# Dense matmuls of a two-layer encoder issued in uninterrupted runs

## The chip, the cores and the metric

The kernel runs on one core of a Trainium2 chip. The metric is device time in microseconds (us) for one execution: the median of three runs of the kernel before is 2465.99 us (2465.27 to 2466.29). Smaller is better.

## The reference

The program is an encoder of two layers over 1024 frames of 1024 channels, in float32. Layer 0 projects the normed input with one matrix (`w_in`), gives one half of the columns to a recurrent mixer (RWKV-7, 8 heads of 64) and the other to a banded attention (8 heads of 64), joins the two and projects back. Layer 1 is a convolution module. Each layer ends in a squared-ReLU feed-forward block (FFN) of width 4096. Cut to what matters here:

```python
h = rmsnorm(x, norm_mix)
proj = h @ w_in                                  # 1024 x 3328
p_rwkv, q, k, v = split(proj)
y = concat([rwkv7_group(p_rwkv, ...), chunk_band_attention(q, k, v, rel_bias)])
x = x + y @ w_out
x = x + square(relu(rmsnorm(x) @ up)) @ down     # 1024 -> 4096 -> 1024
# inside rwkv7_group, one step for each of 1024 frames:
sa = S @ (-kk_t)
S  = S * w_t + outer(sa, kk_t * a_t) + outer(v_t, k_t)
y_t = S @ r_t
```

The feed-forward blocks and the projections are large and independent matmuls. The recurrence is a chain: each block of 64 frames needs the state that the block before it left.

## The kernel before

**Tiles.** Activations lie channel by frame, in tiles of 128 channels by 512 frames, so the 1024 frames are two halves (0 and 1). A product with a weight matrix is made of dense steps, each one matmul of a 128x128 weight block with a 128x512 activation tile. Weights and activations are split in a high and a low part, and `gemm` (L273 to L275) issues three matmuls for each block: high by high, high by low, low by high. One output tile takes 8 blocks, so 24 dense matmuls into one PSUM bank. The column block for the attention's values (L367 to L369) uses four banks at once. In all there are 8,976 dense matmuls; below they are counted from the start of the program.

**Weights.** Each part of four blocks is loaded on SyncE's queue (`wr`, L213), cast on ScalarE (`wh`, L217) and subtracted on VectorE (`wl`, L218). In the mixed stage there are four buffers of each, one part serves 12 dense matmuls.

**The mixed stage.** Mixer and attention consist of small matmuls with ScalarE and VectorE steps between them. They are interleaved on TensorE with dense work that doesn't depend on them. The first part runs mixer and attention of half 0 beside `w_in_gemm` of half 1 (dense matmuls 625 to 1248). The second part runs mixer and attention of half 1 beside `mixer_out` and `ffn` of half 0 (1249 to 2976). Then the pools change and the wide stage begins with `glu`; it holds no mixer and no attention. Before the mixed stage lies `w_in_gemm` of half 0 (1 to 624), with the transposes of the input (L311).

**The mixer's lines.** `prep` (L478 on: low-rank matmuls L481 and L482, head sums L442 and L449, L534, L547), `stage2` (L638, L645, the inverse L609 and L621), and `chain`. Chain does for each 64 frames three matmuls in one bank `c`, each of which needs the one before it by way of ScalarE and VectorE: L667, then `zs` (L669, L670), L671, then `uv` (L672, L673), L677, then the state (L680), and again L667. Then come L687, L691 and `finish` (L442, L449, L713). Attention has L791 and L793 (scores), L813 (transposes) and L820 (values). Results go through DRAM tiles `yd` (L715, L824) and are read by `mixer_out` into `mh` (L867).

**What sets the order.** A scheduler places the instructions of all engines before the program runs. On each engine it takes, of what it holds to be ready, the instruction with the lowest priority number. Each kind of work counts up from a level of its own:

```python
level = {"support": 1_000, "mixer": 1_000_000, "attn": 2_000_000, "dense": 3_000_000}
```

So weight preparation and evacuations (`boost()`) go first, then the mixer, then attention, and a dense matmul is placed only where nothing else is held to be ready. The engines then run these fixed orders; an instruction that isn't ready holds up all that stand behind it on its engine.

Of the kernel before, what the change touches and what calls it, by code (L numbers as in the profile page):

```python
# [14 lines left out]
P = 128  # L15
# [3 lines left out]
KT = 8  # L19
KH = 4  # L20
# [31 lines left out]


LINE = 32


def whole(n):
    return -(-n // LINE) * LINE


@with_exitstack
def encoder_trunk(ctx: ExitStack, tc: tile.TileContext, x, vecs, consts, ext, w2a2, g2, w_in, w_out,
                  up0, dn0, pw1, pw2, up1, dn1, out):
    nc = tc.nc
# [15 lines left out]
    def psum(tag):  # L80
        return ps[tag].tile([P, T], F32, tag=tag, name=tag)
# [53 lines left out]
    yd = [dram.tile([P, SEQ], F32, tag=f"yd{i}", name=f"yd{i}") for i in range(KT)]  # L135
    xd = [[dram.tile([P, T], F32, tag=f"xd{h}_{i}", name=f"xd{h}_{i}") for i in range(KT)] for h in range(2)]

    level = {"support": 1_000, "mixer": 1_000_000, "attn": 2_000_000, "dense": 3_000_000}

    class At:  # L140
        def __init__(self, name):
# [6 lines left out]
        def __exit__(self, *a):  # L148
            level[self.name] = tc.cur_priority
            tc.cur_priority = self.save  # L150

    def boost():
        return At("support")
# [72 lines left out]
    def gemm(w, row0, mts, rhs, evac, st=None, first=(), taper=False, after=None, halves=False):  # L226
        mts = list(mts)
        step = 2 if wide[0] else 1
        units = [(mts[i : i + step], ALL) for i in range(0, len(mts), step)]
        late = st if wide[0] and st is not None and st.r is None else None  # L230
        if late is not None and len(units) > 2:
            units[2:3] = [([m], ALL) for m in units[2][0]]
        if taper:
            cuts = (slice(0, T // 2), slice(T // 2, T)) if halves else (ALL,)
            units[-1:] = [([m], c) for c in cuts for m in units[-1][0]]
        held, late_m, loaded = [], [], {}

        def tail():
            with boost():
                for m, c in late_m:  # L240
                    after(m, c)
            late_m.clear()

        def flush():
            with boost():
                for m, c, q in held:
                    evac(m, q, c)
            held.clear()

        def get(m):  # L250
            if m not in loaded:
                loaded[m] = weights(w, row0, m)
            return loaded[m]

        for i, (grp, cols) in enumerate(units):
            with boost():
                ws = [first[i]] if i < len(first) else [get(m) for m in grp]
            qs = [psum(SPARE[i] if first and i < len(SPARE) else "d") for _ in grp]
            for k in range(KT):
                if i == 1 and k == 6 and late is not None:  # L260
                    with boost():
                        late.spread()
                    flush()
                if k == KT // 2:
                    while deferred:
                        deferred.pop(0)()
                    if late_m:
                        tail()
                xh, xl = rhs[k]
                with At("dense"):  # L270
                    for q, parts in zip(qs, ws):
                        hi, lo = (a[:, k % KH, :] for a in parts[k // KH])
                        nc.tensor.matmul(q[:, cols], hi, xh[:, cols], start=(k == 0), stop=False)  # L273
                        nc.tensor.matmul(q[:, cols], hi, xl[:, cols], start=False, stop=False)  # L274
                        nc.tensor.matmul(q[:, cols], lo, xh[:, cols], start=False, stop=(k == KT - 1))  # L275
            held += [(m, cols, q) for m, q in zip(grp, qs)]
            if i == 0 and late is not None:
                with boost():
                    late.sums()
            else:  # L280
                flush()
            if after is not None:
                late_m += [(m, cols) for m in grp]
        if late_m:
            deferred.append(tail)
# [52 lines left out]
    def w_in_gemm(h, rhs, st, first=()):  # L338
        def evac(m, q, cols):
            rstd = st.rstd()  # L340
            s = tmp("t1")
            if Q0 <= m < K0:
                nc.vector.scalar_tensor_tensor(out=s[:], in0=q[:], scalar=0.125, in1=rstd[:],
                                               op0=ALU.mult, op1=ALU.mult)
            else:
                nc.vector.tensor_tensor(out=s[:], in0=q[:], in1=rstd[:], op=ALU.mult)
            ts = slice(h * T, (h + 1) * T)
            if Q0 <= m < V0:
                hi = tmp("t2")
                nc.scalar.copy(hi[:].bitcast(F32R), s[:])  # L350
                nc.vector.tensor_tensor(out=s[:].bitcast(F32R), in0=s[:], in1=hi[:], op=ALU.subtract)
                nc.gpsimd.dma_start(ph[m][:, ts], hi[:])
                nc.gpsimd.dma_start(pl[m][:, ts], s[:])
            else:
                nc.gpsimd.dma_start(pd[m][:, ts], s[:])

        gemm(w_in, 0, IN_ORDER, rhs, evac, st, first)
        qs = [psum(tag) for tag in SPARE]
        for k in range(KT):
            with boost():  # L360
                hi, lo = (a[:].rearrange("p a b -> p (a b)")
                          for a in weight_part(w_in[k * P : (k + 1) * P, V0 * P : V0 * P + RW], RW))
            xh, xl = rhs[k]
            with At("dense"):
                for t, q in enumerate(qs):
                    ts = slice(t * P, (t + 1) * P)
                    nc.tensor.matmul(q[:], xh[:, ts], hi, start=(k == 0), stop=False)  # L367
                    nc.tensor.matmul(q[:], xl[:, ts], hi, start=False, stop=False)
                    nc.tensor.matmul(q[:], xh[:, ts], lo, start=False, stop=(k == KT - 1))  # L369
        with boost():  # L370
            for t, q in enumerate(qs):
                s = tmp("t1")
                nc.scalar.activation(s[:], q[:], AF.Copy, scale=st.part[1][:, t : t + 1])
                nc.gpsimd.dma_start(vd[h * T + t * P : h * T + (t + 1) * P, :], s[:])
# [487 lines left out]
    def mixer_out(h, xs, mp):  # L862
        with boost():
            rhs = []
            for k in range(KT):
                t = mp.tile([P, T], F32, tag="mh", name="mh")
                nc.sync.dma_start(t[:], yd[k][:, h * T : (h + 1) * T])  # L867
                rhs.append(split(t[:], k))
        st, nrhs, last = norm_collect(xs, "g1")
        residual_gemm(w_out, 0, rhs, xs, last=last)  # L870
        return nrhs, st
# [152 lines left out]
    with banks(d=2, w=2, v=1, c=1, a=2), tc.tile_pool(name="lop", bufs=1) as lop, tc.tile_pool(name="wp1", bufs=4) as wb[0]:  # L1024
# [7 lines left out]
        with tc.tile_pool(name="xrp", bufs=4, reuse_waits="tile") as xrp:  # L1032
# [17 lines left out]
            for i in range(8):  # L1050
                t = dram.tile([P, EXTW + 1], F32, tag=f"ext{i}", name=f"ext{i}")
# [13 lines left out]
        with tc.tile_pool(name="mp", bufs=8, reuse_waits="tile") as mp, tc.tile_pool(name="rp2", bufs=1, reuse_waits="tile") as rp, tc.tile_pool(name="ap2", bufs=1, reuse_waits="tile") as ap:  # L1065
            with At("mixer"):
                rwkv(1, rp, 2)
            with At("attn"):
                attention(1, ap)
            r, s = mixer_out(0, xa, mp)  # L1070
            r, s = ffn(xa, r, s, up0, dn0, mp, "g2")
            stash_x(0, xa)

    wide[0] = True
    with banks(d=5, w=1, o=2), tc.tile_pool(name="wp2", bufs=8, reuse_waits="tile") as wb[0], tc.tile_pool(name="mp2", bufs=10, reuse_waits="tile") as mp, tc.tile_pool(name="sx", bufs=4, reuse_waits="tile") as extra[0], tc.tile_pool(name="up", bufs=1, reuse_waits="tile") as up:
        dwt = up.tile([P, KT * TAPS], F32, tag="dwt", name="dwt")
        nc.scalar.dma_start(dwt[:], vecs[:, VOFF["dw"] : NVEC])
        halo = up.tile([P, KT, TAPS - 1], F32, tag="halo", name="halo")
        nc.gpsimd.memset(halo[:], 0.0)
        us = glu(0, r, s, up)  # L1080
        with At("mixer"):
            ca, sca = conv(us, up)
        with boost():
            xb = fetch_x(1)
        r, s = mixer_out(1, xb, mp)
        r, s = ffn(xb, r, s, up0, dn0, mp, "g2", late=lambda: conv_norm(ca, sca, up))
        stash_x(1, xb)
        us = glu(1, r, s, up)
        with boost():
            xa = fetch_x(0)  # L1090
        r, s = pw2_block(ca, xa)
        with At("mixer"):
            cb, scb = conv(us, up)
        o = Out(0, xa, up, False)
        ffn(xa, r, s, up1, dn1, mp, None, o, late=lambda: conv_norm(cb, scb, up))
        deferred.append(o.finish)
        with boost():
            xb = fetch_x(1)
        r, s = pw2_block(cb, xb)
        ffn(xb, r, s, up1, dn1, mp, None, Out(1, xb, up, True))  # L1100
        deferred.pop()()
# [69 lines left out]
```

## Time and profile before

| | |
|---|---|
| median of three runs | 2465.99 us |
| the profiled execution's own time | 2465.91 us |
| its span (first to last instruction) | 2463.8 us |
| TensorE (PE) busy | 2425.1 us (98%) |
| weight loads on TensorE (PEld) busy | 1963.6 us (80%) |
| VectorE (DVE) busy | 1709.4 us (69%) |
| ScalarE (ACT) busy | 1192.7 us (48%) |
| clock granted to TensorE, mean | 0.996 of full |

All times of the trace count from the start of the span. Dense matmul 625 starts at 235 us, number 1249 at 499 us, 2017 (the first after the last matmul of mixer or attention) at 865 us, and 2977 (the wide stage) at 1083 us. A matmul's bar ends by a model: in a stream of dense matmuls a bar is 0.39 us long and the next one starts 0.23 us after it, so the step from start to start is the time that counts. A matmul of float32 operands shows as two (x2) where it isn't a transpose.

### The profile page before, as it was taken

To read this page: it belongs to the slowest core of one execution; us is meant where nothing else is said; L and a number is where in the kernel's file an instruction comes from. 1 tells how busy PE (TensorE), PEld (TensorE's weight loads), DVE (VectorE), ACT (ScalarE), POOL (GpSimd) and SP (SyncE) were. 2 spreads that over 40 slices of the span, in tenths; PEclk is the share of its full clock that TensorE was granted. 3 is DMA by queue.
4 is the path that set the end of the run, shared out by engine and by line. 5 is a ranking of instruction groups with operands and counts; after the bars stand their busy time and mean duration, and the time that the engine had idled before them with its cause. 6 is when DMAs were issued, how large, how long until landed. Compare 5 with 4: busy or idle time off the path is not lost.

```text
span 2463.8 us, 37387 instructions
## 1 busy us (share of the span) xinstructions
PE 2425.1 (98%) x12972; PEld 1963.6 (80%) x12972; DVE 1709.4 (69%) x3561; ACT 1192.7 (48%) x2288; POOL 109.5 (4%) x251
## 2 busy tenths in 40 slices
PE   8999999999999999999999999999999999999998
PEld 6777777777777788888888888888888888888887
DVE  5688875588876534459999946599998475444444
ACT  5457666477876723343443235434332365433334
POOL 1110011100000000001000000000000000000000
PEclk9999999999999999999999999999999999999999
DMA  8544344632332333363333333533333334333332
GB/s 268 167 148 138 104 127 144 206 111 82 104 98 74 107 96 98 96 208 100 97 94 94 100 98 99 158 94 95 99 95 97 99 98 152 96 94 99 99 94 69
DMA packets 476460, 283.37 MB, mean 115 GB/s; under 512 B 44512, under 2 KB 453472, under 8 KB 476272
## 3 DMA queue, kind: packets, MB, share of 16 engines
q1 hardware_dynamic: 466080, 250.25, 35.0%
q0 software_dynamic: 9152, 29.36, 3.4%
q8 instruction: 102, 1.67, 0.3%
q10 hardware_dynamic: 1040, 1.38, 0.2%
q14 instruction: 86, 0.70, 0.1%
HBM read 247.31 MB, written 36.72 MB: 115 GB/s over the span
## 4 chain that ended last, share of the span: by engine, by line
PE 88%; DVE 4%; DMA 3%; ACT 3%; issue 1%; SPq 1%; ACTq 0%; DVEq 0%
PE d L275 25%; PE d L274 25%; PE d L273 25%; PE a L820 2%; PE w L547 1%; PE v L621 1%; PE a L813 1%; PE a L791 1%; DMA pt<-pd 1%; DVE wl L218 1%; PE c L677 1%; PE c L667 1%; PE c L671 1%; PE a L793 1%; DMA nb<-msc 0%
## 5 line engine op out<-in xcount | busy, mean ns | idle before, releaser
L217 ACT CAST wh<-wr 128x512 fp32r<-128x512 f32 x744 | 460.7, 621 | 955.7 <-PE d L274 876.3
L273 PE MATMUL d<-xh,wh 128*128 128x512 f32 x1872 | 740.6, 396 | 0.6 <-ACT wh L217 0.6
L275 PE MATMUL d<-xh,wl 128*128 128x512 f32 x1872 | 739.4, 395 | 0.9 <-DVE wl L218 0.9
L274 PE MATMUL d<-xl,wh 128*128 128x512 f32 x1872 | 738.6, 395 | 0.0
L218 DVE TENSOR_TENSOR wl<-wr,wh 128x512 fp32r<-128x512 f32 x744 | 501.6, 684 | 237.9 <-ACT wh L217 185.3
L273 PEld LDWEIGHTS d<-xh,wh 128*128 128x128 f32 x1872 | 352.9, 189 | 70.1 <-ACT wh L217 1.0
L275 PEld LDWEIGHTS d<-xh,wl 128*128 128x128 f32 x1872 | 352.7, 188 | 70.2 <-DVE wl L218 1.6
L274 PEld LDWEIGHTS d<-xl,wh 128*128 128x128 f32 x1872 | 353.0, 189 | 69.2 <-issue 1.7
L273 PE MATMUL d<-mh,wh 128*128 128x512 f32 (+1 forms) x1040 | 403.9, 388 | 0.0
L274 PE MATMUL d<-ml,wh 128*128 128x512 f32 (+1 forms) x1040 | 402.8, 387 | 0.0
L275 PE MATMUL d<-mh,wl 128*128 128x512 f32 (+1 forms) x1040 | 402.4, 387 | 0.0
L943 DVE SCALAR_TENSOR_TENSOR cv<-u,dwt,cv 128x512 f32<-128x512 f32 x480 | 331.6, 741 | 0.7
L273 PEld LDWEIGHTS d<-mh,wh 128*128 128x128 f32 x1040 | 195.4, 188 | 38.7 <-issue 0.2
L274 PEld LDWEIGHTS d<-ml,wh 128*128 128x128 f32 x1040 | 195.5, 188 | 38.3
L275 PEld LDWEIGHTS d<-mh,wl 128*128 128x128 f32 x1040 | 195.5, 188 | 38.3
L842 DVE TENSOR_TENSOR x<-d,x 128x512 f32<-128x512 f32 (+1 forms) x146 | 97.6, 678 | 155.0 <-PE d L275 154.7
L884 DVE SCALAR_TENSOR_TENSOR t<-d,rstd 128x512 f32<-128x512 f32 x128 | 86.3, 686 | 112.2 <-PE d L275 109.2
L890 DVE TENSOR_TENSOR ml<-t,mh 128x512 fp32r<-128x512 f32 x128 | 87.7, 687 | 17.9 <-ACT mh L888 15.0
L886 ACT ACTIVATE t<-t 128x512 f32<-128x512 f32 x128 | 80.1, 626 | 14.4 <-DVE t L884 13.9
L888 ACT ACTIVATE mh<-t 128x512 fp32r<-128x512 f32 x128 | 78.8, 616 | 0.0
L184 DVE TENSOR_TENSOR acc<-acc,t 128x512 f32<-128x512 f32 (+1 forms) x86 | 57.8, 673 | 9.7 <-ACT t L183 9.3
L676 ACT ACTIVATE sd<-vs,dc 64x64 f32<-64x64 f32 x128 | 44.2, 345 | 35.4 <-DVE vs L680 29.4
(265 smaller groups left out, 2369.5 us busy)
## 6 DMA issues: line engine op xcount, KB each, us to landing
wr<-in_up_dram SPq DMA_DIRECT2D x256, 256.0 KB
wr<-in_dn_dram SPq DMA_DIRECT2D x256, 256.0 KB
wr<-in_w_in_dram SPq DMA_DIRECT2D x104, 256.0 KB
wr<-in_pw_dram SPq DMA_DIRECT2D x96, 256.0 KB
wr<-in_w_out_dram SPq DMA_DIRECT2D x32, 256.0 KB
pd<-t POOLq DMA_DIRECT2D x28, 256.0 KB, 2.5
x<-xd SPq DMA_DIRECT2D x24, 256.0 KB
pt<-pd SPq DMA_DIRECT2D x42, 128.5 KB
```

What stands on the lines that cost most here:

```text
L184: nc.vector.tensor_tensor(out=self.acc[:, cols], in0=self.acc[:, cols], in1=sq[:, cols], op=ALU.add)
L217: nc.scalar.copy(hi[:], raw[:])
L218: nc.vector.tensor_tensor(out=lo[:], in0=raw[:], in1=hi[:].bitcast(F32), op=ALU.subtract)
L273: nc.tensor.matmul(q[:, cols], hi, xh[:, cols], start=(k == 0), stop=False)
L274: nc.tensor.matmul(q[:, cols], hi, xl[:, cols], start=False, stop=False)
L275: nc.tensor.matmul(q[:, cols], lo, xh[:, cols], start=False, stop=(k == KT - 1))
L842: nc.vector.tensor_tensor(out=xs[m][:, cols], in0=q[:, cols], in1=xs[m][:, cols], op=ALU.add)
L884: nc.vector.scalar_tensor_tensor(out=t[:], in0=q[:], scalar=0.0, in1=rstd[:], op0=ALU.max, op1=ALU.mult)
L886: nc.scalar.activation(sq[:], t[:], AF.Square)
L888: nc.scalar.activation(hi[:], t[:], AF.Square)
L890: nc.vector.tensor_tensor(out=lo[:], in0=sq[:], in1=hi[:].bitcast(F32), op=ALU.subtract)
L943: nc.vector.scalar_tensor_tensor(out=c[:], in0=u[:, tap : tap + T], scalar=dw(tap), in1=c[:], op0=ALU.mult, op1=ALU.add)
```

## The change

Dense matmuls of the mixed stage (and of `w_in_gemm` of half 0) are issued in runs. The first of a run, its head, keeps the lowest priority; the others get the highest, 10, and each carries an order-only dependency on its head, so that none is placed ahead of it. A run has 6 matmuls in `w_in_gemm` (two blocks of one bank) and 12 in `mixer_out` and `ffn` of half 0 (four blocks, one part of weights). In the wide stage a run has one matmul, which is the old rule. Core of the diff:

```diff
+RUN = 6, 12, 6
...
-    level = {"support": 1_000, "mixer": 1_000_000, "attn": 2_000_000, "dense": 3_000_000}
+    level = {"run": 10, "support": 1_000_000, "mixer": 2_000_000, "attn": 3_000_000, "dense": 4_000_000}
...
+    runs = {"n": 0, "size": 1, "head": None}
+
+    def dense(*a, **k):
+        lead = runs["n"] % runs["size"] == 0
+        with At("dense" if lead else "run"):
+            ins = nc.tensor.matmul(*a, **k)
+        if lead:
+            runs["head"] = ins
+        else:
+            tc.add_manual_dep(ins.ins, runs["head"].ins.name,
+                              mybir.DependencyInfo(mybir.DependencyClass.NoSync, mybir.DependencyReason.DATA),
+                              reason="dense steps in runs")
+        runs["n"] += 1
+
+    def run_of(n):
+        runs.update(n=0, size=n)
...
-                with At("dense"):
-                    for q, parts in zip(qs, ws):
-                        hi, lo = (a[:, k % KH, :] for a in parts[k // KH])
-                        nc.tensor.matmul(q[:, cols], hi, xh[:, cols], start=(k == 0), stop=False)
-                        nc.tensor.matmul(q[:, cols], hi, xl[:, cols], start=False, stop=False)
-                        nc.tensor.matmul(q[:, cols], lo, xh[:, cols], start=False, stop=(k == KT - 1))
+                for q, parts in zip(qs, ws):
+                    hi, lo = (a[:, k % KH, :] for a in parts[k // KH])
+                    dense(q[:, cols], hi, xh[:, cols], start=(k == 0), stop=False)
+                    dense(q[:, cols], hi, xl[:, cols], start=False, stop=False)
+                    dense(q[:, cols], lo, xh[:, cols], start=False, stop=(k == KT - 1))
...
+        run_of(RUN[0])
         gemm(w_in, 0, IN_ORDER, rhs, evac, st, first)
+        run_of(RUN[2])
         qs = [psum(tag) for tag in SPARE]
...
+            run_of(RUN[1])
             r, s = mixer_out(0, xa, mp)
...
     wide[0] = True
+    run_of(1)
```

In the changed kernel every dense matmul has the line of the helper, L158; the mixer's lines stand 18 lower in the file (L667 is L685, L671 is L689, L677 is L695, L481 is L499).

**TensorE, first part, one step of the recurrence.** The bank `c_3873` belongs to the last unit of half 0; `d_...` rows are dense. Before:

```order
L667 MATMUL c_3873<-vs_3689,g_3643 128x128
L273 MATMUL d_5357<-xh_4861,wh_5353 128x512
L274 MATMUL d_5357<-xl_4862,wh_5353 128x512
L820 MATMUL a_4486<-pT_4481,vt_4409 64x128
L820 MATMUL a_4486<-pT_4476,vt_4454 64x128
L671 MATMUL c_3873<-zs_3901,xt1_1560 128x64
L820 MATMUL a_4486<-pT_4481,vt_4454 64x128
L791 MATMUL a_4507<-kk_4391,qq_4494 128x384
L793 MATMUL a_4507<-kk_4391,ql_3962 128x384
L275 MATMUL d_5357<-xh_4861,wl_5354 128x512
L273 MATMUL d_5397<-xh_4819,wh_5387 128x512
L677 MATMUL c_3873<-vs_3689,bkt_3688 128x128
```

The same step in the changed kernel:

```order
L689 MATMUL c_3873<-zs_3901,xt1_1560 128x64
L158 MATMUL d_5745<-xh_4843,wh_5741 128x512
L158 MATMUL d_5745<-xl_4844,wh_5741 128x512
L158 MATMUL d_5745<-xh_4843,wl_5742 128x512
L158 MATMUL d_5745<-xh_4849,wh_5741 128x512
L158 MATMUL d_5745<-xl_4850,wh_5741 128x512
L158 MATMUL d_5745<-xh_4849,wl_5742 128x512
L695 MATMUL c_3873<-vs_3689,bkt_3688 128x128
L831 MATMUL a_4739<-cst_75,pt_4718 128x128 x3
L158 MATMUL d_5745<-xh_4855,wh_5741 128x512
```

From L671 to L677 there stood two dense matmuls and three small ones; now six dense ones stand there and nothing else. In the second part it is 12.

**TensorE, the first low-rank matmul of the mixer.** `w_1606` and `w_1607` are its banks, in `w_in_gemm` of half 0; the dense rows beside it work on output tile `d_674`. Before:

```order
L275 MATMUL d_634<-xh_312,wl_631 128x512
L273 MATMUL d_674<-xh_235,wh_664 128x512
L481 MATMUL w_1606<-xl0_1579,lora0_176 128x256
L482 MATMUL w_1606<-xl0_1579,lora2_178 128x256
L274 MATMUL d_674<-xl_236,wh_664 128x512
L481 MATMUL w_1607<-xl1_1582,lora1_177 128x256
```

After the change:

```order
L158 MATMUL d_674<-xl_291,wh_670 128x512
L158 MATMUL d_674<-xh_290,wl_671 128x512
L499 MATMUL w_1606<-xl0_1579,lora0_176 128x256
L500 MATMUL w_1606<-xl0_1579,lora2_178 128x256
L499 MATMUL w_1607<-xl1_1582,lora1_177 128x256
L500 MATMUL w_1607<-xl1_1582,lora3_179 128x256
L158 MATMUL d_674<-xh_301,wh_670 128x512
```

It stood behind the 193rd dense matmul, 65 behind the norm's transposes (L201); now it stands behind the 210th, 78 behind them (L219).

**SyncE's queue, between the two parts.** `yd_131` to `yd_138` hold the results of mixer and attention; `wr` are weights, `pt` is what the mixer of half 1 starts from. Before:

```order
L753 DMA vt<-vd 128x128 x2
L770 DMA qq<-ph_115 64x2x128
L867 DMA mh<-yd_131 128x512
L213 DMA wr<-in_w_in_dram 128x512
L867 DMA mh<-yd_132 128x512
```

After:

```order
L231 DMA wr<-in_w_in_dram 128x512 x2
L231 DMA wr<-in_w_out_dram 128x4x128
L885 DMA mh<-yd_131 128x512
L885 DMA mh<-yd_132 128x512
L885 DMA mh<-yd_133 128x512
L885 DMA mh<-yd_134 128x512
L885 DMA mh<-yd_135 128x512
L885 DMA mh<-yd_136 128x512
L885 DMA mh<-yd_137 128x512
L885 DMA mh<-yd_138 128x512
L231 DMA wr<-in_w_out_dram 128x4x128 x4
L436 DMA pt<-pd_112 128x257
```

The loads of `mh` used to stand behind the first loads of the mixer and attention of half 1; now they stand ahead of them.

**Counts.** Among the first 3,000 dense matmuls, uninterrupted stretches of dense matmuls fall from 400 to 270, and places where a small matmul directly follows a small one of another line rise from 498 to 608. The three steps of the chain occur 190 times; between two of them stand no dense matmul in 18 cases, 1 to 3 in 70, 4 or 5 in 45 and 6 or more in 57 before; none in 43, and 6 or more in 147 after. The last matmul of mixer and attention stood behind dense matmul 2016 and now stands behind 2940; that of half 0 stood behind 1060 and now behind 1176. From dense matmul 2977 on, TensorE's order is the same as before.

More of the change, by code (lines that the diff above doesn't have):

```diff
@@ L363, in w_in_gemm @@
             xh, xl = rhs[k]
[L364 to L369, printed above, removed]
+            for t, q in enumerate(qs):
+                ts = slice(t * P, (t + 1) * P)
+                dense(q[:], xh[:, ts], hi, start=(k == 0), stop=False)
+                dense(q[:], xl[:, ts], hi, start=False, stop=False)
+                dense(q[:], xh[:, ts], lo, start=False, stop=(k == KT - 1))
         with boost():
```

## The prediction

> **What bounds the kernel now.** First the page's line of busy time, then the same by stage. The columns of a stage are busy time of PE, PEld, DVE, ACT and POOL with counts, then granted clock, DMA share and GB/s.
>
> ```profile
> PE 2425.1 (98%) x12972; PEld 1963.6 (80%) x12972; DVE 1709.4 (69%) x3561; ACT 1192.7 (48%) x2288; POOL 109.5 (4%) x251
> ```
>
> ```profile
> 0.00:88.00 88.00, 74.16 (x330) 57.54 (x331) 46.26 (x84) 46.60 (x87) 14.33 (x47) 0.96 0.81 257
> 88.00:470.00 382.00, 375.20 (x2645) 286.81 (x2644) 285.46 (x841) 244.63 (x552) 48.47 (x115) 1.00 0.47 139
> 470.00:850.00 380.00, 370.56 (x2771) 289.50 (x2770) 290.35 (x896) 273.69 (x576) 17.54 (x46) 0.99 0.36 103
> 850.00:1065.00 215.00, 215.00 (x986) 177.30 (x985) 97.01 (x157) 80.10 (x137) 4.77 (x15) 1.00 0.36 104
> ```
>
> TensorE carries the whole kernel. In the mixed stage it shows 382 − 375.2 = 6.8 us and 380 − 370.56 = 9.4 us without a bar, in the dense rest none. So two things can change: what the mixed stage waits, and what it costs to go from dense to small matmuls and back. From dense matmul 2977 on the order on TensorE is unchanged, so I take nothing from there.
>
> Next the waits of TensorE: over the whole span the costliest, then the two largest of each mixed window (total us, times, longest).
>
> ```profile
> PE w L481 <- DVE xl L464: 4.9, 2, 4.1
> ```
>
> ```profile
> PE w L442 <- ACT e L499: 1.3, 1, 1.3
> PE w L449 <- ACT e L447: 1.1, 2, 0.9
> ```
>
> ```profile
> PE c L667 <- DVE vs L680: 1.8, 2, 1.1
> PE v L638 <- DVE bk L528: 1.8, 1, 1.8
> ```
>
> All are small matmuls waiting for the mixer's own steps on ScalarE or VectorE. But bars hide part of it. Here dense matmuls stream, and here one is followed late by the chain's L677 (timeline: start, length):
>
> ```profile
> 880.07 0.39 PE L273 MATMUL d<-mh,wh 128*128 128x512 f32 x1
> 880.30 0.39 PE L274 MATMUL d<-ml,wh 128*128 128x512 f32 x1
> ```
>
> ```profile
> 252.55 0.40 PE L275 MATMUL d<-xh,wl 128*128 128x512 f32 x1
> 252.96 0.49 PE L677 MATMUL c<-vs,bkt 128*128 128x128 f32 x2
> ```
>
> The step is 0.41 us against 0.23, so 0.18 us were lost without any gap between bars. I therefore read steps from start to start. Between 88 and 850 us there are 372 places where a small matmul follows a dense one; first and last:
>
> ```profile
> 89.53 0.39 PE L273 MATMUL d<-xh,wh 128*128 128x512 f32 x1
> 89.77 0.44 PE L449 MATMUL w<-cst,e 128*128 128x128 f32 x2
> ```
>
> ```profile
> 847.08 0.39 PE L273 MATMUL d<-xh,wh 128*128 128x512 f32 x1
> 847.70 0.77 PE L813 MATMUL a<-cst,pt 128*128 128x128 f32 x5 [0.23 <-ACT pt L804]
> ```
>
> Their steps sum to 123.7 us. Taking for each kind of small matmul its quick steps (0.23 to 0.34 us), they would be 96.1. So these places wait 27.6 us, 0.07 us each.
>
> **Part by part.** The order-only dependencies add no instruction, and the matmuls are the same: nothing. *The first wait.* The low-rank matmul L481 waits longest of all:
>
> ```profile
> 70.48 0.39 PE L273 MATMUL d<-xh,wh 128*128 128x512 f32 x1
> 74.95 0.55 PE L481 MATMUL w<-xl,lora 128*128 128x256 f32 x1 [4.08 <-DVE xl L464]
> ...
> 77.22 0.63 PE L274 MATMUL d<-xl,wh 128*128 128x512 f32 x1
> 77.65 0.63 PE L275 MATMUL d<-xh,wl 128*128 128x512 f32 x1
> ```
>
> It now has 78 instead of 65 dense matmuls behind the norm's transposes, 13 x 0.227 = 3.0 us more cover; 1.1 us of the wait stay. Its operand doesn't come later by that: the evacuations that feed it keep their priority. **−3.0** (0 to −4.1).
>
> *The clock.* After that wait dense steps are 0.43 us instead of 0.23, about 12 of them, 2.4 us; the row of the first 88 us has clock 0.96. With 1.1 us of idleness I expect no drop: **−2.4**. The window from 470 has 0.99, up to 3.8 us of lost clock near 478 us, in a stretch of float32 matmuls and waits; half of it goes, **−1.5** (0 to −3.8). [...]
>
> *Fewer changes between dense and small.* One isolated group:
>
> ```profile
> 541.58 0.40 PE L274 MATMUL d<-xl,wh 128*128 128x512 f32 x1
> 541.81 0.38 PE L677 MATMUL c<-vs,bkt 128*128 128x128 f32 x2
> 541.95 0.48 PE L275 MATMUL d<-xh,wl 128*128 128x512 f32 x1
> 542.27 0.39 PE L273 MATMUL d<-xh,wh 128*128 128x512 f32 x1
> ```
>
> L677 takes 0.14 us, and the first dense step behind it 0.32 instead of 0.23: 0.23 us in all. Joined to another group:
>
> ```profile
> 301.90 0.38 PE L677 MATMUL c<-vs,bkt 128*128 128x128 f32 x2
> 302.21 0.87 PE L820 MATMUL a<-pT,vt 128*64 128x128 f32 x10
> ```
>
> ```profile
> 863.37 0.40 PE L275 MATMUL d<-xh,wl 128*128 128x512 f32 x1
> 863.69 1.31 PE L820 MATMUL a<-pT,vt 128*64 128x128 f32 x20
> ```
>
> Now it takes 0.31 us, but L820 no longer follows a dense matmul, whose step is 0.32 instead of 0.23: 0.22 us net. So joining groups saves next to nothing where nothing is waited for. 130 stretches go (400 to 270), I take 0.02 us each: **−3** (+3 to −9, the lower end by the 0.07 us of waiting in each).
>
> *Cover for the chain.* A step from L671 to L677 can be as short as this:
>
> ```profile
> 180.09 0.33 PE L671 MATMUL c<-zs,xt 128*128 128x64 f32 x2
> ...
> 180.97 0.49 PE L677 MATMUL c<-vs,bkt 128*128 128x128 f32 x2
> ```
>
> 0.88 us, against 0.69 for three dense matmuls. Of the 190 chain steps 88 had three or fewer dense ones between; now 43 have none and all others six or more. Taking the chain for the whole, waits fall to 43/88 of 27.6 us: **−14** (0 to −25). The nearest row for the upper end is the chain itself, since steps with none between have attention's work there.
>
> *Small behind small.* 110 more places; their waits aren't listed apart. Between 0 and the 0.07 us of a dense-to-small place I take 0.02: **+2** (0 to +8).
>
> *Between the parts.* SyncE now holds eight `mh` loads ahead of `w_out` weights and of the loads for the mixer of half 1; they wait for the last `yd`. Behind the last small matmul of half 0 (dense 1176) 72 dense ones remain before `mixer_out`, 16.3 us. The store's landing, and the first load of `mh` and first use before:
>
> ```profile
> DMA to landing us min/median/max: 1.8/2.2/4.4
> ```
>
> ```profile
> L867 SPq DMA_DIRECT2D mh<-yd x8: 319/440/1434, 468.6 to 474.4; - x8
> L163 ACT CAST xh<-mh x8: 612/616/619, 473.3 to 499.8; 128x512 fp32r<-128x512 f32 x8
> ```
>
> At most 4.4 + 4.7 us = 9.1: **0**, covered by those 72; without them it would cost up to 9. The same holds at the end: the mixer ends 36 dense matmuls (8 us) before the wide stage, whose first evacuation lies another 48 behind; its tiles overlay the mixer's and wait for its last store on POOL's queue, 2.2 us. **0**.
>
> Sum: −3.0 − 2.4 − 1.5 − 3 − 14 + 2 = −21.9. The profiled execution took 2465.91 us, the median of the runs is 2465.99, so one base serves for both: 2466 − 22 = **2444 us**. A measurement can tell 0.2%, 4.9 us, from no change.
>
> **Rivals.** *Waits only move* (16%). Longer runs don't help if what is late is a queue on VectorE, or if waits reappear between small matmuls. For it: VectorE is 75 to 76% busy in the mixed windows. Against: the chain's cover triples. Then only the first wait and the joining count: −6, 2460 us.
>
> *Runs starve* (7%), the slower one. A run once begun can't be filled with other work if its `wl` or `wh` is late. The casts:
>
> ```profile
> L218 DVE TENSOR_TENSOR wl<-wr,wh 128x512 fp32r<-128x512 f32 x146 | 99.5, 682 | 29.3 <-ACT wh L217 28.0 <-PE d L275 0.4 <-issue 0.2
> L217 ACT CAST wh<-wr 128x512 fp32r<-128x512 f32 x145 | 89.2, 616 | 54.6 <-PE d L274 44.2 <-PE a L368 8.5 <-DMA vt<-vd 1.3
> ```
>
> The mixed stage now holds 193 parts of weights (dense 625 to 2940 by 12). 0.11 us late in each eats the gain; at 0.2 us it is +39 − 22 = +17, 2483 us. Against: ScalarE waits 44 us for TensorE to free a buffer, so weights are ahead, and the next part comes with 36 dense matmuls (8 us) to spare.
>
> *Much more is hidden* (5%). Weight loads fill 75 and 76% of the mixed windows but 82% of the dense one; at that share 576 us of loads take 699 instead of 762 us. If two thirds of these 63 us came back the time would be 2424 us. Against: the joined group above saves nothing. [...]
>
> *Nothing changes* (4%): the new order waits elsewhere for what it saves, 2466 us. That runs aren't formed at all the order excludes.
>
> **How the numbers follow.** My forecast has 68%. Its own range is 2430 to 2458: the chain's term, between −3 and −25, moves it by 11 us either way, the other terms by some 3 more. With waits that only move it reaches 2462, and a part of the hidden room takes the lower end to 2428. Faster by over 0.2% (below 2461): 68 + 5 + 10 of the 16 = 83%; within: 4 + 6 = 10%; slower: 7%.
>
> **What would show it.** Right: dense matmul 2977 starts near 1061 us instead of 1083; L481's wait is near 1 us and no 0.43 us steps follow; the chain's rows (L667, L671) leave the list of waits; the small-to-dense steps are unchanged. Wrong: dense rows (L158) with idle time put to `wh` or `wl`, waits of small matmuls for each other as large as before, or a gap at the two ends of half 0.

## The result and the profile after

| | before | after |
|---|---|---|
| median of four runs each, us | 2466.14 (2465.27 to 2467.04) | 2441.29 (2440.69 to 2441.99) |
| the profiled execution's own time, us | 2465.91 | 2441.99 |
| its span, us | 2463.8 | 2440.2 |
| clock granted to TensorE, mean | 0.996 | 0.997 |
| dense matmul 2977 starts at, us | 1082.7 | 1058.8 |

The change makes the kernel faster by 24.85 us. The ratio is 0.9899, with a 95% interval of 0.9882 to 0.9916, so 21 to 29 us. The forecast was 2444. Of all the executions below one stands apart: the kernel with runs of 4 took 9449 us once, at a mean clock of 0.53, and the ratios leave it out.

First the page's line of busy time for the kernel after, then its windows by stage (length; busy time of PE, PEld, DVE, ACT and POOL with counts; clock, DMA share, GB/s). The last window ends 3 us behind the start of the wide stage.

```profile
PE 2408.0 (99%) x12972; PEld 1970.2 (81%) x12972; DVE 1710.8 (70%) x3561; ACT 1183.8 (49%) x2282; POOL 113.4 (5%) x251
```

```profile
0.00:88.00 88.00, 74.56 (x332) 57.32 (x333) 46.16 (x84) 46.16 (x87) 14.26 (x47) 0.96 0.81 255
88.00:470.00 382.00, 377.97 (x2678) 297.98 (x2677) 283.63 (x829) 237.14 (x536) 48.22 (x111) 1.00 0.46 137
470.00:850.00 380.00, 374.60 (x2488) 308.08 (x2487) 273.25 (x776) 256.48 (x521) 14.96 (x44) 1.00 0.42 118
850.00:1062.00 212.00, 210.73 (x1319) 170.86 (x1319) 128.26 (x306) 106.66 (x218) 9.84 (x25) 1.00 0.34 99
```

Time without a bar on TensorE in the two mixed windows falls from 6.8 and 9.4 us to 4.0 and 5.4, some 7 us. That is less than a third of the gain; the rest lay under the bars, as the prediction said. The first row is what it was: 74.56 us busy at clock 0.96, against 74.16 at 0.96.

The largest waits of TensorE in the kernel after (total us, times, longest), first two between 88 and 470 us, then three between 470 and 1062:

```profile
PE c L689 <- ACT zs L688: 1.2, 4, 0.4
PE v L627 <- DVE e L621: 0.8, 2, 0.5
```

```profile
PE w L499 <- ACT e L442: 2.9, 1, 2.9
PE c L695 <- ACT vs L691: 1.0, 3, 0.6
PE d L158 <- DVE wl L236: 0.9, 1, 0.9
```

The chain (L689, L695) is still in the list, with 0.3 us at a time. The longest wait of the mixed stage is now that of a low-rank matmul at the start of the second part, 2.9 us.

What the waiting lists can't show is the step under a bar. One chain step of the kernel after (start, length):

```profile
250.07 0.39 PE L158 MATMUL d<-xh,wl 128*128 128x512 f32 x1
250.30 0.33 PE L689 MATMUL c<-zs,xt 128*128 128x64 f32 x2
250.44 0.48 PE L158 MATMUL d<-xh,wh 128*128 128x512 f32 x1
...
251.68 0.40 PE L158 MATMUL d<-xh,wl 128*128 128x512 f32 x1
251.91 0.38 PE L695 MATMUL c<-vs,bkt 128*128 128x128 f32 x2
```

Six dense matmuls stand between L689 and L695, and both small matmuls start 0.23 us after the dense one ahead, the step of an undisturbed stream. In the step that the prediction shows of the kernel before, L677 (now L695) came 0.41 us behind. The first dense matmul behind the group still takes its longer step: 0.31 us at 250.44.

So the whole stretch from TensorE's first matmul to dense 2977 can be divided, step by step from start to start. *Entry* is the step from a dense matmul to the small one behind it, less 0.228 us, the mean step of undisturbed dense matmuls. *Exit* is the first dense step behind a small matmul, less 0.228. *Body* is the step of each small matmul up to the next start. All are sums in us, worked out from the start times of the two traces:

| | before | after | difference |
|---|---|---|---|
| entry to the chain's three matmuls | 11.4 | 2.8 | −8.6 |
| entry to attention | 9.1 | 0.3 | −8.8 |
| entry to the rest of the mixer and the norm's sums | 17.9 | 8.9 | −9.0 |
| exits from these three | 22.3 | 18.2 | −4.1 |
| bodies of these three | 299.5 | 300.3 | +0.8 |
| low-rank matmuls, transposes of input and norm | 37.2 | 38.3 | +1.1 |
| dense steps themselves | 681.9 | 686.8 | +4.9 |

The sum is −23.7 us; dense 2977 starts 23.9 us earlier, as TensorE's first matmul comes 0.1 us sooner. The gain is in the entries of all three kinds. The chain has nearly as many of them as before (129 against 135), and each waits less. Attention has hardly any left (14 against 102), since its matmuls now mostly follow other small ones. Not all of an entry is waiting: some small matmuls start no sooner than 0.31 us behind a dense one (34 of L639 in the kernel after, median 0.32). Set against the quick steps of each kind, as in the prediction, the waits from 88 us on fall from some 30 us to some 8; some 3 us more are entries that are gone.

### The profile page after: what moved, and what is told of

The parts are those of the page before. It is cut to its first block, busy times and chain, and to the rows that moved or that the text cites. A ratio compares the mean times of both kernels' runs of the same rounds, so it can differ in the third digit from the quotient of the medians.

```text
span 2440.2 us, 37269 instructions
## 1 busy us (share of the span) xinstructions
PE 2408.0 (99%) x12972; PEld 1970.2 (81%) x12972; DVE 1710.8 (70%) x3561; ACT 1183.8 (49%) x2282; POOL 113.4 (5%) x251
## 4 chain that ended last, share of the span: by engine, by line
PE 87%; DVE 4%; DMA 3%; issue 3%; ACT 2%; SPq 0%; POOL 0%; ACTq 0%; DVEq 0%; POOLq 0%
PE d L158 76%; PE w L565 1%; PE a L838 1%; PE v L639 1%; PE a L831 1%; DVE wl L236 1%; PE a L809 1%; PE c L685 1%; PE c L695 1%; DMA xd<-xo 1%; DMA pt<-pd 1%; PE a L811 1%; PE c L689 1%; DMA wr<-in_w_in_dram 0%; PE w L552 0%
## 5 line engine op out<-in xcount | busy, mean ns | idle before, releaser
L158 PE MATMUL d<-xh,wh 128*128 128x512 f32 x1872 | 746.1, 399 | 1.9 <-ACT wh L235 1.3
L158 PE MATMUL d<-xh,wl 128*128 128x512 f32 x1872 | 732.3, 391 | 0.9 <-DVE wl L236 0.9
L158 PE MATMUL d<-xl,wh 128*128 128x512 f32 x1872 | 732.1, 391 | 0.0
L158 PEld LDWEIGHTS d<-xh,wl 128*128 128x128 f32 x1872 | 352.7, 188 | 77.3 <-DVE wl L236 1.6
L158 PEld LDWEIGHTS d<-xh,wh 128*128 128x128 f32 x1872 | 353.0, 189 | 73.6 <-issue 2.2
L158 PEld LDWEIGHTS d<-xl,wh 128*128 128x128 f32 x1872 | 353.2, 189 | 68.0 <-issue 0.5
L158 PE MATMUL d<-mh,wh 128*128 128x512 f32 (+1 forms) x1040 | 407.2, 392 | 0.0
L158 PE MATMUL d<-mh,wl 128*128 128x512 f32 (+1 forms) x1040 | 402.0, 386 | 0.0
L158 PE MATMUL d<-ml,wh 128*128 128x512 f32 (+1 forms) x1040 | 401.6, 386 | 0.0
L158 PEld LDWEIGHTS d<-mh,wl 128*128 128x128 f32 x1040 | 195.3, 188 | 40.3
L158 PEld LDWEIGHTS d<-ml,wh 128*128 128x128 f32 x1040 | 195.5, 188 | 37.6
L158 PEld LDWEIGHTS d<-mh,wh 128*128 128x128 f32 x1040 | 195.4, 188 | 37.7 <-issue 0.2
L904 ACT ACTIVATE t<-t 128x512 f32<-128x512 f32 x128 | 80.0, 625 | 12.2 <-DVE t L902 11.9
```

Source lines behind the costliest of these rows:

```text
L158: ins = nc.tensor.matmul(*a, **k)
L904: nc.scalar.activation(sq[:], t[:], AF.Square)
```

## The experiments

Four theories are named. COVER: a longer run gives the steps on ScalarE and VectorE time to finish before TensorE asks for them. BREAKS: each stretch of dense matmuls that goes saves a fixed cost. STARVING: long runs wait for weights. SUPPLY was formed after the second run: a small matmul that isn't ready is passed by a whole run, so long runs use up the dense work of a part before its mixer ends. RUN gives the run lengths in `w_in_gemm`, in `mixer_out` and `ffn` of half 0, and in the column block of values. Each kernel was timed beside the kernel before; medians and ratios:

| RUN or kernel | us | before | ratio (95%) |
|---|---|---|---|
| 3, 3, 3 | 2462.09 | 2466.22 | 0.9987 (0.9978 to 0.9996) |
| 6, 24, 6 | 2526.44 | 2466.22 | 1.025 (1.0236 to 1.0264) |
| before with longer chain | 2475.4 | 2466.22 | 1.004 (1.0028 to 1.0053) |
| after with longer chain | 2451.04 | 2466.22 | 0.9945 (0.9933 to 0.9957) |
| 6, 6, 6 | 2445.21 | 2466.03 | 0.9921 (0.9906 to 0.9935) |
| 1, 12, 1 | 2447.28 | 2466.03 | 0.9933 (0.9918 to 0.9948) |
| 6, 1, 6 | 2460.19 | 2466.03 | 0.9983 (0.9974 to 0.9993) |
| 12, 12, 12 | 2501.06 | 2466.03 | 1.014 (1.0119 to 1.0161) |
| 6 in half 0's `w_in_gemm` alone | 2464.16 | 2466.47 | 0.9995 (0.9985 to 1.0004) |
| 4, 12, 4 | 2450.37 | 2466.47 | 0.9942 (0.9929 to 0.9956) |
| 5, 12, 6 | 2440.06 | 2466.47 | 0.9901 (0.9887 to 0.9915) |
| 6, 10, 6 | 2452.12 | 2466.47 | 0.995 (0.9936 to 0.9963) |

**Runs of three.** Three dense matmuls last 0.69 us, less than a step of the chain (0.88 us).

```diff
-RUN = 6, 12, 6
+RUN = 3, 3, 3
```

> Runs of 3 in every stage. In its order 327 stretches of dense matmuls remain up to dense 2976 (before 399, changed kernel 269), and of the chain's steps 103 have three or fewer dense matmuls between (before 88, changed 43). Theory COVER (the gain is that the chain's step of 0.88 us is covered by 1.38 us of dense work): three dense matmuls are 0.69 us and cover nothing, so waits stay near 28 us and only joining is left: 2457 to 2466 us. Theory BREAKS (each stretch saved is worth 25/130 = 0.19 us, waits or not): 72 fewer, -14, 2452 us.

Dense stretches fall from 399 to 327 (up to dense 2976), but only 4.1 us are gained. Entries to chain, attention and mixer fall by 13.6 us, but the bodies grow by 4.9 and the dense steps by 3.6: much of the waiting has only moved. BREAKS is out in the form that a stretch is worth a fixed sum: the first 72 stretches less bring 4 us, the next 58 (269 in the kernel after) some 21.

**Runs of 24 in the second part.**

```diff
-RUN = 6, 12, 6
+RUN = 6, 24, 6
```

> Runs of 6 in the first part, 24 (a whole output tile, two parts of weights) in the second. 208 stretches remain. COVER: 6 and 12 cover already, so nothing more to win: 2438 to 2446 us, as the changed kernel; the mixer now ends with dense 2976, so if anything later. BREAKS: 191 fewer than before, -36, 2430 us. STARVING (a run can't be filled when its weights are late): a run now spans two parts of weights, dense rows show idle time put to wh or wl, slower than the changed kernel by 5 us or more.

Neither theory saw 60 us of loss. Dense matmul 2900 starts at 978.2 us, 60.5 earlier than in the kernel after (1038.7), because small work that used to stand ahead of it now stands behind; 2977 starts only at 1142.1. Between dense 2976 and 2977 stand 348 small matmuls. Windows of this kernel, then its three largest waits on TensorE between 980 and 1137 us, then a piece of its timeline:

```profile
900.00:980.00 80.00, 79.65 (x441) 66.33 (x437) 47.40 (x120) 45.46 (x88) 3.77 (x7) 1.00 0.43 123
1000.00:1137.00 137.00, 94.94 (x660) 71.81 (x658) 67.40 (x223) 48.41 (x124) 4.01 (x9) 0.58 0.07 18
```

```profile
PE c L685 <- DVE vs L698: 7.3, 10, 1.1
PE c L689 <- ACT zs L688: 5.6, 10, 0.7
PE c L695 <- ACT vs L691: 5.3, 10, 0.6
```

```profile
1059.69 0.42 PE L695 MATMUL c<-vs,bkt 128*128 128x128 f32 x1
1060.78 0.80 PE L685 MATMUL c<-vs,g 128*128 128x128 f32 x2 [0.68 <-DVE vs L698]
1062.13 0.69 PE L689 MATMUL c<-zs,xt 128*128 128x64 f32 x2 [0.55 <-ACT zs L688]
1063.37 0.79 PE L695 MATMUL c<-vs,bkt 128*128 128x128 f32 x2 [0.55 <-ACT vs L691]
```

While dense work lasts, TensorE is full (79.65 of 80 us). Then only small matmuls are left, in places the chain alone with one matmul each 1.1 to 1.4 us, with DMA at 7% and the clock at 0.58. The loss is at the end of the part and not in the runs, so STARVING is out here too: dense matmuls wait 1.4 us for `wh` and `wl` in the whole kernel, and none of it there. This is what SUPPLY was formed from.

**A longer chain, in the kernel before and after.** The two copies of `zs` go through another tile, one more step on VectorE and ScalarE in each block of 64 frames; what is computed stays the same.

```diff
+z0 = rp.tile([P, C], F32, tag="z0", name="z0", bufs=1)
-nc.vector.tensor_copy(zs[hs[0], :], zp[...])
-nc.scalar.copy(zs[hs[1], :], zp[...])
+nc.vector.tensor_copy(z0[hs[0], :], zp[...])
+nc.scalar.copy(z0[hs[1], :], zp[...])
+nc.vector.tensor_copy(zs[hs[0], :], z0[hs[0], :])
+nc.scalar.copy(zs[hs[1], :], z0[hs[1], :])
```

> The kernel before with one more copy in each of the chain's 64 steps from L667 to L671 (zs is copied through a second tile, on VectorE and ScalarE as before), about 0.3 us more latency; TensorE's work is the same. COVER: its chain is already short of cover, so part of 64 x 0.3 us comes on top: 5 to 15 us slower than before. BREAKS: latency doesn't matter, within 3 us of before.

> The changed kernel with the same added copy in each of 64 chain steps. COVER: runs of 12 (2.7 us) have room for it and runs of 6 (1.38 us against 0.88 + 0.3) just so: at most 4 us slower than the changed kernel, so the gap between the two lengthened kernels is wider than 25 us. BREAKS: within 3 us of the changed kernel, the gap stays at 25 us.

The kernel before loses 9.2 us. So does the one after: 9.8. By the totals COVER failed. The parts differ, though. (Their small work ahead of dense 1249 is the same or nearly so, so they can be compared.) From dense 1249 to 2977 the kernel before grows from 583.0 to 587.9 us, the one after doesn't (578.9 to 576.7), as COVER has it. In the first part the lengthened kernel after is level up to dense 1200 (466.9 and 468.0 us), and then takes 24.7 us to dense 1250 instead of 12.2: there the last matmul of the mixer of half 0 starts at 480.0 us instead of 461.7 and stands behind dense 1242 of 1248. Its largest waits between 220 and 440 us, where the chain of half 0 runs, and between 440 and 500:

```profile
PE c L692 <- ACT zs L691: 0.5, 1, 0.5
```

```profile
PE a L812 <- ACT t L391: 2.6, 2, 2.4
PE d L158 <- ACT xh L181: 2.1, 1, 2.1
```

`xh` is cast from `mh`, the results of mixer and attention. The mixer's last store to `yd` is issued at 481.5 us, the loads of `mh` follow from 484.8, the first cast comes at 490.2 and the second part's first dense matmul at 490.9 (in the kernel after the loads start at 466.0, the cast at 469.5 and that matmul at 479.9). The clock is at half for 10.2 us from 486.3 us instead of 3.4 us from 492.7 (from 440 to 500 us it is 0.91 in the mean, 0.97 in the kernel after). In the kernel before with the same edit one matmul of the chain (L671, there L674) waits far more over the span than without it (1.7 us), where the lengthened kernel after has 1.6:

```profile
PE c L674 <- ACT zs L673: 5.3, 13, 0.7
```

Part of its 9.2 us is the clock as well: half clock covers 27.3 us up to dense 2977 instead of 13.7 (mean clock 0.994 against 0.996), which by half of the difference is worth up to 6.8. So by these traces a longer step is covered where dense work is left, and shows where it is nearly used up; the totals alone don't say so.

**Which part gains.** Three kernels: runs of 6 throughout, runs in the second part alone, runs in the first part alone.

```diff
-RUN = 6, 12, 6
+RUN = 6, 6, 6
```

```diff
+RUN = 1, 12, 1
```

```diff
+RUN = 6, 1, 6
```

> Runs of 6 in every stage. 277 stretches remain (changed kernel 269), 40 chain steps with three or fewer dense matmuls (changed 43), and the mixer of half 1 ends behind dense 2370 instead of 2940. COVER: six dense matmuls (1.38 us) cover a step of 0.88 us, so nearly the whole gain: 2440 to 2448 us. BREAKS: 8 stretches more than the changed kernel, 2443 us. Should VectorE be late more often than the bare step says, 6 is too little and the second part gives back part of its gain: 2450 us.

> Runs only in the second part (12); start and first part as before. COVER: the second part's share of the waits, 13 to 16 us less than before: 2450 to 2453 us. BREAKS: 65 of 130 stretches go, -12: 2454 us. If runs in one part are paid for in the other, the two halves (this one and the next) don't add up to -25 us.

> Runs only in the start and the first part (6); second part as before. COVER: the first part's share of the waits and 1 to 3 us of the first wait, 8 to 12 us less than before: 2454 to 2458 us. BREAKS: 79 of 130 stretches go, -15: 2451 us.

By the medians the second part gains 18.75 us and all before it 5.8, together 24.6, the whole change; by the ratios it is 16.5 and 4.2, and their intervals allow sums from 15 to 27. That the parts add up is thus shown only so far. Of the 18.75 us some 2.1, by its trace, lie ahead of dense 1249, where TensorE's order is that of the kernel before. Runs of 6 in both gain 20.8, most of what 12 brings. From 3 to 6 the gain rises from 4 to 21 us, while the stretches go from 327 to 277: run length decides, somewhere near the duration of a chain step, as COVER has it. In the runs of 6 the entries to chain, attention and mixer are 15.1 us (24.8 with three, 12.0 in the kernel after), and the bodies 303.9 (304.4; 300.3).

**Runs of 12 in the first part as well.**

```diff
-RUN = 6, 12, 6
+RUN = 12, 12, 12
```

> Runs of 12 in every stage. 230 stretches remain, 39 fewer than in the changed kernel. Theory SUPPLY (a chain step takes a whole run, so the mixer can outlast the dense work of its part, and then nothing covers it): in this order 168 small matmuls of half 0 stand behind the first part's last dense matmul and 31 of half 1 behind the second's, so TensorE idles with a low clock at both places: 15 to 40 us slower than the changed kernel, 2456 to 2481 us. BREAKS: 39 fewer, -7, 2434 us. COVER alone: the same as the changed kernel.

This was to test SUPPLY: the first part has 624 dense matmuls. It came out as SUPPLY said and worse than its numbers. 168 small matmuls stand behind dense 1248, and dense 1249 starts at 549.3 us instead of 479.9. Window and the two largest waits on TensorE of this kernel up to there:

```profile
400.00:549.00 149.00, 118.10 (x824) 89.03 (x824) 70.46 (x266) 79.75 (x184) 13.96 (x35) 0.78 0.30 92
```

```profile
PE v L467 <- ACT e L465: 8.6, 3, 3.5
PE a L831 <- ACT pt L822: 4.1, 6, 1.8
```

The second part then takes less than in the kernel after, but most of the 69 us stay lost.

**The start alone.** Runs of 6 only in `w_in_gemm` of half 0, the old order from there on, to price the terms on the first wait and the clock behind it.

```diff
-RUN = 6, 12, 6
+RUN = 6, 1, 6
...
-        run_of(RUN[0])
+        run_of(RUN[0] if h == 0 else 1)
...
-        run_of(RUN[2])
+        run_of(RUN[2] if h == 0 else 1)
```

> Runs of 6 only in w_in_gemm of half 0 (dense 1 to 624); the mixed parts keep single placement. The first low-rank matmul stands behind dense 210 as in the changed kernel. If the first wait and the clock behind it are worth what the prediction says, 3 to 6 us less than before: 2460 to 2463 us. If the wait moves along with its operand and the clock drops all the same, within 2 us of before.

Nothing that can be measured (−2.3 us by the medians, −1.2 by the ratio, interval −3.7 to +1.0). The granted clock still drops to half at 55.4 and 79.3 us, for 3.4 us each; the dense steps from 55.54 to 58.10 us and from 80.10 are 0.43 us.

**Neighbours of the chosen lengths.** Is there a better pair, and is the curve smooth?

```diff
+RUN = 4, 12, 4
```

```diff
+RUN = 5, 12, 6
```

```diff
+RUN = 6, 10, 6
```

> Runs of 4 in the first part, 12 in the second. 51 chain steps of the first part have 4 or 5 dense matmuls between (0.92 us, just the 0.88 of a bare step), the mixer of half 0 ends behind dense 1108 instead of 1176 and that of half 1 behind 2844 instead of 2940. COVER: a bare step has no room for a queue, 2 to 5 us slower than the changed kernel, 2443 to 2446 us. SUPPLY: more dense work is left at the boundary, whose 2.9 us wait and clock drop may go: up to 4 us faster, 2437 us.

> Runs of 5 in the first part (runs then end inside a block), 12 in the second. The mixer of half 0 ends behind dense 1124, that of half 1 behind 2844. 1.15 us of cover against 0.88. Between the changed kernel and 3 us faster: 2438 to 2442 us.

> Runs of 6 and 10 (ends inside a block). 255 stretches, 14 fewer than in the changed kernel, 48 short chain steps (43), the mixer of half 1 ends behind dense 2558. COVER: 2.3 us are as good as 2.7, the time of the changed kernel within 2 us. BREAKS: -3, 2438 us. Between the runs of 6 (2445 us) and 12 (2441 us) on a smooth curve it would be 2442 us.

Five is as good as six. Four costs 9 us, in COVER's direction but more than it said, and the trace puts the loss at another place: one group of attention at the end of the first part. The largest wait on TensorE from 440 to 500 us in the kernel with 4, and its timeline there:

```profile
PE a L831 <- ACT pt L822: 5.6, 3, 3.6
```

```profile
463.98 0.40 PE L811 MATMUL a<-kk,ql 128*128 128x512 f32 x1
467.99 1.76 PE L831 MATMUL a<-cst,pt 128*128 128x128 f32 x7 [3.61 <-ACT pt L822]
```

5.6 us of waits, and from 466.6 us on 6.8 us at half clock (the dense bar at 471.28 us is 0.63 us long, elsewhere 0.39), which by half of that can cost up to 3.4: these two can make up the 9 us without the chain, whose entries (2.3 us against 2.8) are no longer than in the kernel after. In the first part alone these are 2.0 us (1.5 in the kernel after, 4.2 before), so four dense matmuls, 0.92 us, already do most of it for a bare step of 0.88 us. In the order of this kernel, attention's last groups stand between two dense matmuls (1176 and 1177) with nothing to cover them.

Ten in the second part costs 11 us, and no theory had that. The entries are as in the kernel after (11.8 against 12.0 us); the bodies are 10.9 us longer (311.2 against 300.3). So small matmuls wait for each other more. Part of it the trace shows: 1.4 us of idle time ahead of L639 at 554 us, 1.1 ahead of L809 at 493.8, and half clock for 17.1 us instead of 10.2 (0.99 in the mean from 470 to 850 us against 1.00), worth up to 3.4. Why ten does that, and twelve doesn't, these runs don't settle. No run is clearly better than the change.

## Why the prediction was right, and where it was not

| term | predicted | measured |
|---|---|---|
| first wait | −3 | about 0 |
| clock after it, and near 478 us | −3.9 | −1.7 at most |
| fewer changes | −3 | −4.1 (exits) |
| cover for the chain | −14 | −26.4 (entries of all three kinds, some 3 of it fewer entries) |
| small behind small | +2 | +0.8 (bodies) |
| between the parts and at the end | 0 | +1 to +3 |

**The mechanism was right, its size was not.** "Taking the chain for the whole" scaled 27.6 us of waits by the chain's steps and left 43/88 of them. The chain's entries alone went from 11.4 to 2.8 us; but attention's went from 9.1 to 0.3 and the rest of the mixer's from 17.9 to 8.9, and those were never chain steps. Attention now mostly follows other small work, and as the bodies hardly grew it seldom waits there either. The waits in entries were the pool, and more than two thirds of it went, not half. The rival "waits only move" is seen in part: bodies grow by 4.9 us in runs of three and by 4.4 in runs of six throughout, there against 23.3 us less in the entries. In the kernel after it is 0.8. Of the prediction's signs dense 2977 near 1061 us came (1058.8), and so did unchanged steps from small to dense. The chain's matmuls stay in the list of waits (L667 had 1.8 us and has 0.5, L671 1.7 and 1.2; L677 has more, 1.0 against 0.2), and the signs on the first wait didn't come.

**The first wait failed.** The prediction took the operand to come when it did ("its operand doesn't come later by that"). Timeline of the kernel after:

```profile
53.92 1.05 PE L208 MATMUL c<-ones,acc 128*128 128x1 f32 x8 [1.51 <-DVE acc L202]
...
79.69 0.55 PE L499 MATMUL w<-xl,lora 128*128 128x256 f32 x1 [2.10 <-DVE xl L482]
...
80.70 0.63 PE L158 MATMUL d<-xh,wh 128*128 128x512 f32 x1
81.13 0.63 PE L158 MATMUL d<-xl,wh 128*128 128x512 f32 x1
```

The matmul started 4.7 us later than before (74.95) and still waited 2.10 us, so its operand came later as well. Of the 4.7 us 3.8 were there at the norm's transposes (59.26 us, before 55.45). Counted from these, TensorE's cover grew by 2.9 us, as forecast, but the operand came 0.9 us later, so the wait itself fell by 2.0. And part of that stands elsewhere: the norm's matmul L208 waits 1.51 us (0.6 before, there L190). All waits of TensorE that the trace lists for the first 88 us sum to 13.7 us before and 13.0 after. The experiment on the start alone finds no gain.

**The clock failed with it.** Dense steps of 0.43 us follow the wait (80.70 to 81.13), where none were forecast. Half clock covers 3.4 us at each of 55.8, 79.7 and 492.7 us, 10.2 in all, instead of 6.8 at 74.2 and 6.8 at 477.0; 3.4 us less of it is by half at most 1.7 us of dense work. The prediction's "With 1.1 us of idleness I expect no drop" had no row behind it, and no run shows its −2.4: here a wait of 2.10 us, and one of 2.08 with the start alone, has the 0.43 us steps behind it, and with the 3.4 us at 55.8 the first 88 us hold 6.8 us of half clock as before. Its "half of it goes" was an estimate as well; the later stretch is 3.4 us long instead of 6.8, but behind another wait, of 2.87 us. Nor does the order alone set the clock: the kernel with runs in the second part alone has TensorE's order of the kernel before up to dense 1249, and its trace shows half clock for 3.4 us there (at 76.2), not 13.7. The mean clock of its profiled execution is 0.998, that of the kernel before 0.996, and the single executions of the kernel before go from 0.995 to 0.998. So this term can't be read from one trace of each kernel.

**Fewer changes** came close, and the added price was right: an exit costs what it did (0.300 against 0.306 us as a step from 88 us on). There are just fewer of them, 252 instead of 285. **Small behind small** came near: the bodies grew by 0.8 us.

**Between the parts** wasn't free. SyncE's `mh` loads themselves are covered (issued 466.0 to 470.6 us; the second part's first dense matmul starts at 479.9), but the first dense matmul of the second part comes 0.99 us after the one ahead, and the low-rank matmul at 491.2 us waits 2.87 us, where its like waited 0.8 before. That is 0.8 and 2.1 us. **The end** held: the mixer ends at dense 2940 of 2976 and TensorE is full up to 2977 (window 850 to 1062, 210.73 of 212 us). But the prediction's 36 dense matmuls to spare were taken to be a comfortable cover for the stage behind. That they are also the margin of the whole change wasn't seen: runs twice as long cost 85 us more than the change.

**Starving** (7%) isn't there. The dense groups of the kernel after, with the idle time before them behind the second bar:

```profile
L158 PE MATMUL d<-xh,wh 128*128 128x512 f32 x1872 | 746.1, 399 | 1.9 <-ACT wh L235 1.3
L158 PE MATMUL d<-xh,wl 128*128 128x512 f32 x1872 | 732.3, 391 | 0.9 <-DVE wl L236 0.9
L158 PE MATMUL d<-xl,wh 128*128 128x512 f32 x1872 | 732.1, 391 | 0.0
```

2.2 us for weights in the whole kernel: 0.9 after the start of the wide stage, 1.3 in the first 88 us. Of the 4.9 us that dense steps take more in the table, 2.0 are steps at half clock, which before fell in good part on small matmuls, and 0.6 are single steps such as the one between the parts. The other 2.4 us are spread thin (0.2293 against 0.2283 us for a step); their cause was not looked for. **Much more hidden** (5%) isn't excluded as such: entries of 12 us and exits of 18 are still there.

Up to dense 2977 the measured 23.9 us stand against 21.9. Entries, exits and bodies brought 14.7 us more than forecast (29.7 against 15), and the start, the clock, the border of the parts and the dense steps some 13 less. That the sum came out near is these two errors cancelling.

## What to carry to other kernels

Where a serial chain shares an engine with independent work, give each of its steps one uninterrupted run as long as the step's detour over the other engines; here six dense matmuls (1.4 us) bring most of it, three (0.69 us) little, 4 of 25 us. Then count: each step that isn't ready spends a whole run, so steps times run length must fit into the independent work of that part, and the margin (36 of 1728 dense matmuls here) is the first thing to look at. Where bars overlap, as those of 0.39 us that start every 0.23 us do here, read waits from start to start: of this gain of 24.85 us only some 7 showed as gaps between bars.

## What the runs showed of the hardware

In the kernel before the granted clock is 0.50 for 6.8 us from 74.2 us and for 6.8 us from 477.0, in the kernel after for 3.4 us from each of 55.8, 79.7 and 492.7, apart from the last stretch of each, which runs into the trace's end. Dense steps at this clock take 0.43 us instead of 0.23. In the kernel after the drops follow single waits of 1.51, 2.10 and 2.87 us (up to 53.92, 79.69 and 491.20 us), with small matmuls around them; in the kernel before the first comes within a wait of 4.08 us (up to 74.95), the second behind one of 1.76 us (up to 475.48, ahead of L638).

The length of a wait alone doesn't account for this. The kernel before also waits 1.61 us up to 505.84 us, ahead of L791, and its clock from 500 to 520 us is 1.00; the kernel after waits 1.51 us up to 53.92 and is at 0.50 from 55.8 to 59.2. What else counts these runs don't settle.

In the tail of the kernel with runs of 24 bars, mostly of small matmuls, cover 94.94 of 137 us, and the granted clock over these 137 us is 0.58.
